# The order in which sixteen experts are traced: the next expert's gate and up products between the steps of the present one's activation

## The chip, the cores and the metric

One program runs on one core of a Trainium2 chip. The metric is the device time of one execution in microseconds. Lower is better.

## What is computed

The reference is a trunk of two layers over 512 tokens of width 1024. Each layer has a mixer (attention and a state space scan in layer 0, a chunked mLSTM in layer 1), a layer norm, a mixture of experts and a second layer norm. The change lies in the mixture and in the norm behind it:

```python
def hier_moe(x, w_group, b_group, w_expert, b_expert, w_gate, w_up, w_down):
    ...
    # one of 4 groups, then the best 2 of its 4 experts, weights normalised
    combine = jnp.einsum('tk,tke->te', weights, one_hot(expert_id, 16))
    hid = silu(einsum('td,edf->tef', t, w_gate)) * einsum('td,edf->tef', t, w_up)
    hid = hid * combine[:, :, None]
    return einsum('tef,efd->td', hid, w_down)

h = layer_norm(DN_ALPHA * h + ffn, ln_g[layer, 1], ln_b[layer, 1])   # DN_ALPHA = 4 ** 0.25
```

An expert has a hidden width of 256. All matrices are f32. The kernel splits each operand into a high and a low part, and a product is three matmuls (high with high, high with low, low with high).

## The kernel before

Each matrix of weights is cut into pieces of 128 x 2048 f32, 1 MB. An expert has three: piece 3e (gate and up columns, first half of the 1024 inputs), piece 3e+1 (second half) and piece 3e+2 (down). `load_piece` brings a piece by one DMA from SP's queue into a staging buffer (`raw`, `raw2`, or one of two `ca`), ScalarE (ACT) casts it to the high part (L213), and VectorE (DVE) or GpSimd (POOL) subtracts to get the low part (L214). Both parts lie in one of two pairs of slots `wh`/`wl` or one of two pairs `x8`/`x8`. `moe_piece(base, i, j)` picks these by the place j in the order of use: the pair by j mod 2; the staging buffer in the cycle raw, ca, ca (`raw2` for j = 3). POOL gets the subtraction by the piece's number i, not by its place: down pieces (i mod 3 = 2) below 42, and pieces 42 and 45.

`route` ranks the experts for one block of 128 tokens at a time, four blocks in all, with a chain of small DVE instructions (L897 to L963). While it works on the last block, the first four pieces of the mixture are already loaded and split, in the gaps of the engines' queues. Piece 2 is the third of them (j = 2) and so POOL's.

`experts` then loops over the 16 experts. Tokens of an expert are collected by a product with a 0/1 matrix, the dispatch, for a pair of experts at a time in four steps of 16 matmuls (`pair_parts`, L1070). A step fills one of the two PSUM buffers `tp`, which ACT (cast) and DVE (subtraction) then empty into `s2` or `xr`. An expert's work as it is traced:

- `gate_up(e)`: pieces 3e and 3e+1, 24 matmuls into a PSUM buffer `pj`
- two of the four dispatch steps of the next pair
- `hidden`: tanh on ACT (L1025), two DVE instructions (L1026, L1027), two transposes on TensorE (L1030) into `sm`
- the split of the transposed hidden values into two `pt` buffers (L213 on ACT, L214 on DVE)
- piece 3e+2 and 12 down matmuls into two `mm` buffers, ACT scales by the routing weight (L1177), ACT's queue writes the rows to `yd` in HBM (L1181)

Experts 14 and 15 stay on chip and are added by matmuls with transposed masks (L1279). After expert 13's write, `gather` makes alpha times x1 in `xr` out of its two parts (L1193 on ACT, L1194 on DVE) and issues eight indirect DMAs from POOL, which fetch the rows of the other experts and add them to `xr` (L1198). Then follow L1281 (adds the product of 14 and 15) and the layer norm (`ln_sums`).

A planner turns the traced program into one fixed order for each engine: at each moment of its own simulated time it takes, of the instructions that are ready, the one that was traced first. What the engines then do late by its reckoning, the queue behind it does late too.

Of the kernel before, what the change touches and what calls it, by code (L numbers as in the profile page):

```python
# [9 lines left out]
F32 = mybir.dt.float32  # L10
# [3 lines left out]
AF = mybir.ActivationFunctionType  # L14
# [6 lines left out]
EPS = 1e-5  # L21
# [30 lines left out]
class Trunk:  # L52
# [249 lines left out]
    def ln_sums(self, y, s, gb, pool):  # L302
# [13 lines left out]
        V.tensor_scalar(ve, ve, EPS, None, op0=ALU.add)  # L316
# [567 lines left out]
    def route(self, tb, layer, gb, lT, mu, rs, first):  # L884
# [78 lines left out]
        V.tensor_scalar(se, se, es, None, op0=ALU.mult)  # L963
# [57 lines left out]
    def hidden(self, gu):  # L1021

        nc = self.nc
        th = self.t("t", [128, 256])
        nc.scalar.activation(th, gu[:, 0:256], AF.Tanh, scale=0.5)  # L1025
        nc.vector.scalar_tensor_tensor(th, th, 1.0, gu[:, 0:256], op0=ALU.add, op1=ALU.mult)  # L1026
        nc.vector.scalar_tensor_tensor(th, th, 0.5, gu[:, 256:512], op0=ALU.mult, op1=ALU.mult)  # L1027
        tp = self.p("sm", [128, 2, 128])
        for k in range(2):
            nc.tensor.transpose(tp[:, k, :], th[:, k * 128:(k + 1) * 128], self.ident)  # L1030
        return tp
# [93 lines left out]
    def experts(self, layer):  # L1125
# [16 lines left out]
        def gate_up(e):  # L1142
            es = slice((e % 2) * 128, (e % 2 + 1) * 128)
            gus[e] = gu = self.p("pj", [128, 512])
            for q in range(2):
                w = self.moe_piece(base, 3 * e + q, next(used))
                for k in range(4):
                    xk = xs[e // 2][q * 4 + k]
                    self.mm3(gu, xk, w, q == 0 and k == 0, q == 1 and k == 3, np.s_[:, es], np.s_[:, k, :])

        for e in range(16):
# [3 lines left out]
            if e < 15:  # L1155
                gate_up(e)
            if e == 14:
                gate_up(15)
            for _ in range(2):
                next(prep, None)  # L1160
            tp = self.hidden(gus.pop(e))
            hT = (self.t("pt", [128, 2, 128], F32R), self.t("pt", [128, 2, 128], F32R))
            self.split(hT[0], hT[1], tp)
            w = self.moe_piece(base, 3 * e + 2, next(used))
# [22 lines left out]

    def gather(self):

        nc = self.nc  # L1190
        for tb in range(4):
            self.xr[tb] = self.t("xr", [128, 1024])
            nc.scalar.activation(self.xr[tb], self.xs[tb][0].bitcast(F32), AF.Copy, scale=ALPHA)  # L1193
            nc.vector.scalar_tensor_tensor(self.xr[tb], self.xs[tb][1].bitcast(F32), ALPHA, self.xr[tb],  # L1194
                                           op0=ALU.mult, op1=ALU.add)
# [400 lines left out]
```

## Time and profile before

| | us |
|---|---|
| median of 3 runs | 1133.4 (1129.15 to 1139.74) |
| profiled execution, its own time | 1130.67 |
| its span, first to last instruction | 1128.9 |
| mean granted TensorE clock over the span | 0.962 |

The profiled execution is the one whose rows are shown below; times in rows are microseconds from the start of the span. In the engine names PE is TensorE's matmul and PEld its weight load.

### The profile page before, as it was taken

The numbers are of one execution on the slowest core, as the hardware profiler recorded it, in microseconds if no ns is written. First come the engines' busy times: TensorE is split into PE (matmuls) and PEld (weight loads), VectorE is DVE, ScalarE is ACT, GpSimd is POOL, SyncE is SP. The second block draws the span as 40 slices with busy tenths as digits, with TensorE's granted clock in tenths as the row PEclk, the third lists the DMA queues.
The fourth block names the chain that finished last, engine by engine and source line by source line (L and its number), as shares of the span: only waits on it lengthen the run. The fifth ranks groups of instructions, "written<-read, shape, count | busy, mean of one in ns | idle before, by whom it ended". The sixth has DMA issues, their size and how long they took to land. (4 is left out here: it accounts for less than half of the span.)

```text
span 1128.9 us, 14811 instructions
## 1 busy us (share of the span) xinstructions
PE 1020.7 (90%) x5522; PEld 826.5 (73%) x5522; DVE 817.8 (72%) x1483; ACT 559.3 (50%) x778; POOL 394.6 (35%) x228
## 2 busy tenths in 40 slices
PE   8879999999979999987699999999999799999872
PEld 6576767767768877775577989898777688878761
DVE  7886899688776766667665766667988767667666
ACT  5223554461446666564544444444424467656644
POOL 3177545001343333346233333331014333424352
PEclk9889999999989999998898999999999899999986
DMA  6313321441356887768622222221413468868685
GB/s 227 109 55 111 122 74 37 171 168 39 117 191 244 302 291 260 278 217 248 140 75 75 76 75 75 75 75 38 150 38 138 149 244 314 291 220 311 224 219 135
DMA packets 48347, 180.62 MB, mean 160 GB/s; under 512 B 17588, under 2 KB 18516, under 8 KB 32264
## 3 DMA queue, kind: packets, MB, share of 16 engines
q1 hardware_dynamic: 41240, 156.11, 39.5%
q0 software_dynamic: 2992, 8.77, 4.0%
q10 hardware_dynamic: 4032, 14.68, 3.2%
q8 instruction: 46, 0.75, 0.3%
q14 instruction: 37, 0.30, 0.1%
HBM read 155.94 MB, written 22.42 MB: 158 GB/s over the span
## 5 line engine op out<-in xcount | busy, mean ns | idle before, releaser
L214 POOL TENSOR_TENSOR wl<-ca,wh 128x2048 fp32r<-128x2048 f32 x18 | 85.0, 4722 | 118.8 <-ACT wh L213 104.8
L265 PE MATMUL pj<-x,wh 128*128 128x512 f32 x288 | 116.8, 406 | 7.4 <-ACT x L213 5.5
L214 POOL TENSOR_TENSOR wl<-raw,wh 128x2048 fp32r<-128x2048 f32 x15 | 69.9, 4663 | 138.2 <-ACT wh L213 138.2
L266 PE MATMUL pj<-x,wh 128*128 128x512 f32 x288 | 115.7, 402 | 0.0
L213 ACT CAST wh<-raw 128x2048 fp32r<-128x2048 f32 (+1 forms) x49 | 88.2, 1800 | 54.6 <-DMA raw<-in_w 41.7
L267 PE MATMUL pj<-x,wl 128*128 128x512 f32 x288 | 115.1, 400 | 0.0
L1070 PEld LDWEIGHTS tp<-t,a 128*128 128x128 f32 x896 | 110.8, 191 | 3.0 <-ACT pt L1062 0.6
L1070 PE MATMUL tp<-t,a 128*128 128x256 f32 x896 | 111.8, 283 | 0.0
L214 POOL TENSOR_TENSOR x<-ca,x 128x2048 fp32r<-128x2048 f32 x14 | 64.5, 4610 | 125.8 <-ACT x L213 92.5
L214 DVE TENSOR_TENSOR wl<-raw,wh 128x2048 fp32r<-128x2048 f32 (+1 forms) x34 | 72.7, 2140 | 43.0 <-ACT wh L213 43.0
L1177 ACT ACTIVATE a<-mm,s5bc 128x512 f32<-128x512 f32 x56 | 38.5, 687 | 72.7 <-PE mm L267 72.7
L213 ACT CAST x<-ca 128x2048 fp32r<-128x2048 f32 (+1 forms) x40 | 66.1, 1652 | 11.5 <-DMA ca<-in_w 7.5
L214 DVE TENSOR_TENSOR wl<-ca,wh 128x2048 fp32r<-128x2048 f32 x12 | 27.5, 2293 | 59.7 <-ACT wh L213 59.7
L265 PEld LDWEIGHTS pj<-x,wh 128*128 128x128 f32 x288 | 55.4, 192 | 19.5 <-ACT x L213 6.3
L266 PEld LDWEIGHTS pj<-x,wh 128*128 128x128 f32 x288 | 55.1, 191 | 12.0 <-DVE x L214 1.6
L267 PEld LDWEIGHTS pj<-x,wl 128*128 128x128 f32 x288 | 55.2, 192 | 10.6
L213 ACT CAST wh<-ca 128x2048 fp32r<-128x2048 f32 x30 | 57.1, 1903 | 8.1 <-DMA ca<-in_w 7.8
L1051 DVE TENSOR_SCALAR t<-iota,rcm 128x128 fp32r<-128x128 f32 x112 | 57.2, 555 | 1.0 <-DMA cd<-rse,rpos 0.9
L280 POOL TENSOR_TENSOR lnrs<-lnve,nhalf 128x1 f32<-128x1 f32 x16 | 13.1, 818 | 125.7 <-DVE lnve L291 99.7
L266 PE MATMUL pj<-wl,x 128*128 128x256 f32 x192 | 56.2, 293 | 0.9 <-DVE wl L214 0.9
L265 PE MATMUL pj<-wh,x 128*128 128x256 f32 x192 | 56.3, 293 | 0.0
L267 PE MATMUL pj<-wh,x 128*128 128x256 f32 x192 | 56.1, 292 | 0.1
(488 smaller groups left out, 2880.5 us busy)
## 6 DMA issues: line engine op xcount, KB each, us to landing
raw<-in_w SPq DMA_DIRECT2D x63, 1024.0 KB, 5.5
ca<-in_w SPq DMA_DIRECT2D x62, 1024.0 KB, 5.7
yd<-a ACTq DMA_DIRECT2D x28, 512.0 KB
a<-in_ln SPq DMA_DIRECT2D x8, 512.0 KB, 6.4
a<-in_w SPq DMA_DIRECT2D x6, 512.0 KB, 6.5
yd<-t SPq DMA_DIRECT2D x6, 512.0 KB, 3.0
ca<-in_xT SPq DMA_DIRECT2D x8, 256.0 KB, 5.5
xr<-in_x SPq DMA_DIRECT2D x4, 512.0 KB, 6.3
```

What stands on the lines that cost most here:

```text
L213: a = nc.scalar.copy(h, src)
L214: b = (eng or nc.vector).tensor_sub(l, src, h.bitcast(F32))
L265: nc.tensor.matmul(ps, lhsT=aH[ai], rhs=bH[bi], start=first, stop=False)
L266: nc.tensor.matmul(ps, lhsT=aH[ai], rhs=bL[bi], start=False, stop=False)
L267: nc.tensor.matmul(ps, lhsT=aL[ai], rhs=bH[bi], start=False, stop=last)
L280: self.last_pow = self.nc.gpsimd.tensor_tensor(rs, ve, self.nhalf, op=ALU.pow)
L1051: ins = nc.vector.tensor_scalar(oh[:, j, m * 128:(m + 1) * 128], self.iota1, c[2 * i + j], None, op0=ALU.is_equal)
L1070: nc.tensor.matmul(tp[:, k, :], lhsT=self.xs[tb][i][:, cs], rhs=ohs[tb], start=tb + i == 0, stop=tb + i == 4)
L1177: nc.scalar.activation(yo[:, ns], ps, AF.Copy, scale=c)
```

## The change

The loop is traced in another order. At expert e the activation of e (L1025 to L1027) comes first, then dispatch steps of the next pair (three at even e, one at odd e), then the first half of `gate_up(e + 1)`, then the transposes and the split for e, the second half of `gate_up(e + 1)`, and the down product of e. The pieces are loaded in the order 0, 1, 3, 4, 2, 6, 7, 5, 9 and so on. x1 is rejoined from its two parts by one DVE addition per block, two traced at expert 12 and two at expert 13, without alpha; the routing weights are divided by alpha instead, and the norm's epsilon by alpha squared.

```diff
-        V.tensor_scalar(ve, ve, EPS, None, op0=ALU.add)
+        V.tensor_scalar(ve, ve, EPS / ALPHA ** 2, None, op0=ALU.add)
...
-        V.tensor_scalar(se, se, es, None, op0=ALU.mult)
+        V.tensor_scalar(se, se, es, 1.0 / ALPHA, op0=ALU.mult, op1=ALU.mult)
...
     def hidden(self, gu):
+        return self.hidden_T(self.hidden_act(gu))
+
+    def hidden_act(self, gu):
...
+        return th
+
+    def hidden_T(self, th):
         tp = self.p("sm", [128, 2, 128])
...
             for q in range(2):
+                if q:
+                    yield
                 w = self.moe_piece(base, 3 * e + q, next(used))
...
-            if e < 15:
-                gate_up(e)
-            if e == 14:
-                gate_up(15)
-            for _ in range(2):
+            if e == 0:
+                list(gate_up(0))
+            th = self.hidden_act(gus.pop(e))
+            for _ in range(1 if e % 2 else 3):
                 next(prep, None)
-            tp = self.hidden(gus.pop(e))
+
+            ahead = gate_up(e + 1) if e < 15 else iter(())
+            next(ahead, None)
+            tp = self.hidden_T(th)
             hT = (self.t("pt", [128, 2, 128], F32R), self.t("pt", [128, 2, 128], F32R))
             self.split(hT[0], hT[1], tp)
+            list(ahead)
+            if e in (12, 13):
+                for tb in (2 * e - 24, 2 * e - 23):
+                    self.rejoin(tb)
             w = self.moe_piece(base, 3 * e + 2, next(used))
...
+    def rejoin(self, tb):
+        self.xr[tb] = self.t("xr", [128, 1024])
+        self.nc.vector.tensor_tensor(self.xr[tb], self.xs[tb][0].bitcast(F32), self.xs[tb][1].bitcast(F32), op=ALU.add)
+
     def gather(self):
         nc = self.nc
-        for tb in range(4):
-            self.xr[tb] = self.t("xr", [128, 1024])
-            nc.scalar.activation(self.xr[tb], self.xs[tb][0].bitcast(F32), AF.Copy, scale=ALPHA)
-            nc.vector.scalar_tensor_tensor(self.xr[tb], self.xs[tb][1].bitcast(F32), ALPHA, self.xr[tb],
-                                           op0=ALU.mult, op1=ALU.add)
```

## Rows read from the trace of the kernel before

**Rows 1.** The page, part 1: busy us, share of the span, instructions of each engine.

```profile
PE 1020.7 (90%) x5522; PEld 826.5 (73%) x5522; DVE 817.8 (72%) x1483; ACT 559.3 (50%) x778; POOL 394.6 (35%) x228
```

**Rows 2.** One expert as a window: length, busy us (instructions) by engine, clock, DMA, GB/s.

```profile
353.70:366.10 12.40, 12.40 (x71) 10.66 (x70) 6.56 (x8) 7.78 (x9) 4.62 (x1) 1.00 0.72 242
```

**Rows 3.** TensorE's waits in layer 0's mixture: us in total, times, longest.

```profile
PE mm L267 <- DVE pt L214: 4.9, 3, 2.1
...
PE sm L1030 <- DVE t L1027: 3.9, 3, 1.7
```

**Rows 4.** Timeline of TensorE, both layers: start us, us, line, tiles, count, [idle before].

```profile
327.76 3.98 PE L1070 MATMUL tp<-t,a 128*128 128x256 f32 x32
...
331.72 0.48 PE L265 MATMUL pj<-x,xr 128*128 128x512 f32 x1
...
337.41 0.40 PE L265 MATMUL pj<-wh,xr 128*128 128x512 f32 x1
...
340.21 3.98 PE L1070 MATMUL tp<-t,a 128*128 128x256 f32 x32
...
488.44 1.03 PE L1059 MATMUL tp<-ident,t 128*128 128x128 f32 x8
...
502.69 3.98 PE L1070 MATMUL tp<-t,a 128*128 128x256 f32 x32
...
890.91 3.98 PE L1070 MATMUL tp<-t,a 128*128 128x256 f32 x32
...
1065.24 3.98 PE L1070 MATMUL tp<-t,a 128*128 128x256 f32 x32
```

**Rows 5.** Timeline of the last block's routing, layer 0, then layer 1.

```profile
306.91 2.29 DVE L214 TENSOR_TENSOR x<-ca,x 128x2048 fp32r<-128x2048 f32 x1
307.27 6.32 POOL L214 TENSOR_TENSOR wl<-ca,wh 128x2048 fp32r<-128x2048 f32 x1 [1.84 <-DMA cd<-rse,rpos]
...
309.11 4.57 DVE L906 TENSOR_TENSOR rgt<-rlg 128x80 bf16<-128x80 f32 x1
...
871.45 0.23 DVE L906 TENSOR_TENSOR rgt<-rlg 128x80 bf16<-128x80 f32 x1
...
871.88 5.17 DVE L908 TENSOR_TENSOR req<-req,low 128x80 bf16<-128x80 bf16 x1
872.47 4.51 POOL L214 TENSOR_TENSOR wl<-ca,wh 128x2048 fp32r<-128x2048 f32 x1
```

**Rows 6.** Timeline around expert 13 and the gather, layer 0, then layer 1.

```profile
501.94 4.80 DVE L1194 SCALAR_TENSOR_TENSOR xr<-a,xr 128x1024 f32<-128x1024 f32 x1 [5.82 <-ACT xr L1193]
...
514.36 1.90 ACT L213 CAST x<-ca 128x2048 fp32r<-128x2048 f32 x1
...
516.88 0.33 ACTq L1181 DMA_DIRECT2D yd<-a  x1
...
1079.42 0.33 ACTq L1181 DMA_DIRECT2D yd<-a  x1
...
1110.34 0.69 DVE L1281 SCALAR_TENSOR_TENSOR xr<-pj,xr 128x512 f32<-128x512 f32 x1 [0.73 <-DMA xr<-yd,rsrc]
```

**Rows 7.** Timeline of one staging buffer that carries down pieces, layer 0.

```profile
384.13 4.61 POOL L214 TENSOR_TENSOR x<-ca,x 128x2048 fp32r<-128x2048 f32 x1 [8.37 <-ACT x L213]
...
388.77 4.35 SPq L247 DMA_DIRECT2D ca<-in_w  x2
...
396.93 4.62 POOL L214 TENSOR_TENSOR wl<-ca,wh 128x2048 fp32r<-128x2048 f32 x1 [8.19 <-ACT wh L213]
```

**Rows 8.** Timeline of the emptying of two dispatch steps, layer 0.

```profile
343.20 0.69 DVE L214 TENSOR_TENSOR s<-tp,s 128x512 fp32r<-128x512 f32 x1
...
458.04 3.98 PE L1070 MATMUL tp<-t,a 128*128 128x256 f32 x32
...
463.16 1.90 ACT L213 CAST x<-ca 128x2048 fp32r<-128x2048 f32 x1 [2.30 <-DMA ca<-in_w]
...
465.57 1.29 DVE L214 TENSOR_TENSOR xr<-tp,xr 128x512 fp32r<-128x512 f32 x2 [1.89 <-ACT xr L213]
```

More of the change, by code (lines that the diff above doesn't have):

```diff
@@ L1027, in hidden @@
         nc.vector.scalar_tensor_tensor(th, th, 0.5, gu[:, 256:512], op0=ALU.mult, op1=ALU.mult)
+        return th
+    def hidden_T(self, th):
         tp = self.p("sm", [128, 2, 128])
         for k in range(2):
-            nc.tensor.transpose(tp[:, k, :], th[:, k * 128:(k + 1) * 128], self.ident)
+            self.nc.tensor.transpose(tp[:, k, :], th[:, k * 128:(k + 1) * 128], self.ident)
         return tp
```

## The prediction

> **What bounds the kernel now.** I read the page first: TensorE is busy for 90% of the span [rows 1], so whatever gains must remove its idle time, or a chain on which it waits. Next I asked where that idle time lies. The windows show an expert without a stall: 12.40 us, all of it busy [rows 2]. TensorE's timeline gives the same work as it comes in practice. From the first dispatch of the loop to expert 13's, 13 experts, layer 0 takes 502.69 - 327.76 = 174.93 us and layer 1 takes 1065.24 - 890.91 = 174.33 [rows 4]. Thirteen unstalled experts are 13 x 12.40 = 161.2, and the last pair adds 1.03 for its transposed masks [rows 4]. So stalls and the refilling after them cost **12.7 us in layer 0 and 12.1 in layer 1**. The waits name their cause: TensorE wants the hidden values split (pt) or the activation done (t) and DVE is late [rows 3].
>
> Then I looked at the end of each mixture. From expert 13's write to the last gathered block in layer 1 is 1110.34 - 1079.42 = 30.9 us [rows 6]; TensorE has less left to do than that. So what counts at the end of a mixture is the moment of expert 13's write.
>
> Last, the routing of the fourth block, ahead of each mixture, is a chain of DVE instructions of which one is far too long: L906 takes 4.57 us in layer 0 and 0.23 in layer 1, where its like L908 takes 5.17 [rows 5]. Each of the long ones ends with POOL's subtraction for piece 2 (307.27 + 6.32 = 313.59; 872.47 + 4.51 = 876.98). DVE stood still while POOL worked.
>
> **The change, part by part.**
>
> *Routing.* The third piece loaded is now piece 3, which is not POOL's. Piece 2 comes as the fifth, when its slot is freed by expert 0's first products, behind the routing. That takes 4.57 - 0.23 = 4.34 us off the chain in layer 0 and 5.17 - 0.23 = 4.94 in layer 1 [rows 5], together 9.3. But DVE now has a subtraction of 2.29 us more at this time. The second piece's already stands in the middle of the chain (306.91, [rows 5]), since the planner fills gaps with what is ready. If piece 3's falls there too, it costs 2 x 2.29 = 4.6; if it falls behind the chain, nothing. I have no row that decides, and take half: **-7.0, bounds -9.3 to -4.7**.
>
> The Trainium skill, Perfetto Trace Analysis, section Optimizing Scalar/DVE Operations, speaks against this part: VectorE and GpSimd share a read port of SBUF, so shifting work between them might not help. By that rule this term would be 0 and the sum -9.8. The rows agree that the two engines hold each other up, but also show that the price here is POOL's whole instruction against DVE's shorter one.
>
> *The stalls between the steps.* The activation of e is now followed on TensorE by the down product of e - 1, one or three dispatch steps and half of the next gate and up product before the transposes. Twelve matmuls take 340.21 - 337.41 = 2.80 us [rows 4], a dispatch step 3.98 / 2 = 1.99 [rows 4]. Thus T(e), the transposes, come at least 2.80 + 1.99 + 2.80 = 7.6 us after the activation can start; that wait should vanish. The split of the hidden values has the second half, 2.80 us, as its cover, and the waits for it were 4.9 in all, three times [rows 3]; I leave 0.5 us of them per layer.
>
> Two new limits come instead.
>
> First, at even e three dispatch steps follow each other through two PSUM buffers. The third waits until the first is emptied, and has the 1.99 us of the second step for it. A quick emptying ends 343.20 + 0.69 - (340.21 + 1.99) = 1.7 us after its step [rows 4, 8]: no wait. A slow one starts at 465.57 and ends about 6.2 us after its step (458.04 + 1.99), since ACT stood behind a cast that waited for a load [rows 8]: a wait of 4.2. These are the fastest and slowest kind of the 14 first steps of layer 0; I worked out all from the timeline, and the mean excess over 1.99 is 1.1 us. With seven pairs that is 7.9 per layer, unless the planner, seeing the buffer full, runs the gate and up matmuls first. I take half, **4.0 per layer (0 to 7.9)**.
>
> Second, the loads. A down piece holds its staging buffer for a load, a cast, POOL's subtraction. Before, in one `ca`, that cycle was 396.93 - 384.13 = 12.80 us, of which the next load started (388.77) as POOL ended (388.74) [rows 7]. Now all down pieces go through the single `raw`. The cycle is as long, but an unstalled expert is 12.40, so it falls behind by 0.4 x 13 = 5.2 us over a layer, and the slot for down piece e is now free only when `gate_up(e)` is done, which leaves a lead of 2.8 + 2.0 + 5.6 + 0.3 - 6.6 = 4 us at odd e (down product, dispatch, products, transposes, less cast and POOL). Lead and lag nearly cancel; with some late landings I take **3 us per layer (0 to 22, the rival below)**.
>
> Left of the 24.8 us: 2 x (0.5 + 4.0 + 3.0) = 15.0. Gain **-9.8, bounds -23.8 to +19**.
>
> *Expert 13's write.* Before, 13 or so of expert 14's 24 matmuls ran ahead of the write; now all must, 11 more at 2.80 / 12 = 0.233: +2.6 us. Against this, the stretch from dispatch to write was 516.88 - 502.69 = 14.19 [rows 4, 6], and now it is dispatch and transposes 4.0, products 5.6, down 2.8, scaling and issue 1.0 (516.88 - 514.36 - 1.90 = 0.6, [rows 6], and the way from the last matmul) = 13.4. The cast of 1.90 us in ACT's queue ahead of the last scaling [rows 6] may return. I take **0, bounds -0.8 to +1.2 per layer**. Behind the write the gather is as it was.
>
> *Rejoining.* Four ACT instructions go, and four DVE instructions are replaced by four of one size. The first took 4.80 [rows 6], again behind POOL, and held up the activation of 13, a wait that is part of the 12.7. Now the additions lie at 12 and 13, behind the products that read the same `xr` buffers, with a whole expert until the gather. A second factor in one tiny instruction and another constant cost nothing: same count and shapes.
>
> *Sum.* -7.0 - 9.8 + 0 = -16.8. The profiled execution takes 1130.67, so 1113.9 by its own time. It lies 2.7 below the median of the runs, within their spread; on the median's scale 1133.4 - 16.8 = **1116.6, said as 1117**.
>
> **The rivals.**
>
> *All is covered.* The planner hides the third step, the loads keep up, the moved subtraction lies behind the routing: -23.8 - 9.3 - 1.6 = -34.7, 1099. For it: 13 of TensorE's experts could run at 12.40. Against: every engine's queue is fixed by planned times, and DVE is held by POOL's 4.6 us once per expert. Band 1099 to 1110.
>
> *The third step eats the gain.* 7.9 instead of 4.0, and 5 instead of 3 for the loads, per layer: stalls left 2 x 13.4 = 26.8, so +2.0, and with a routing gain of 4.7 to 7.0 the time is 1128 to 1131. For it: the mean of the rows as they are.
>
> *The loads become the bound (slower).* One `raw` for down pieces, with POOL's subtraction inside its cycle. If landing and waiting for the cast grow by 1.7 us, the cycle is 14.5 against 13.46 per expert now (174.93 / 13, [rows 4]): 13 x 1.04 = 13.5, less the lead of about 4, +9.5 per layer; with the routing's -7 that is +12, 1145. It decides from a cycle of some 13.9 on. For it: ACT's cast was seen to wait 2.30 us for a load [rows 8]. Against: the same cycle was run at 12.80 before.
>
> *The change does not do what it says.* The planner already starts the next products while the present activation waits (331.72, before expert 0's down product, [rows 4]). If its order hardly changes, only the routing's part is left: -4.7 to -9.3, 1124 to 1129.
>
> *The routing gains nothing.* By the mechanism that DVE is busy where POOL was: -9.8, 1123.6.
>
> **How the numbers follow.** Forecast (1110 to 1122) 0.42; all covered 0.12; third step 0.20; loads 0.10; order unchanged 0.10; no gain in routing 0.06. About 1% is what a measurement of this kernel can tell from no change: faster is below 1122.1, slower above 1144.7. Faster: 0.42 + 0.12 and a little of the rest, 0.56. Slower: half of the loads' case and some chance for what I didn't see, 0.08. The range for 8 in 10 leaves out the best of the covered case and the loads' case: 1101 to 1138.
>
> **What would show it.** In the changed profile: L906 and L908 of the last block at about 0.2 us each, no subtraction on POOL beside them, and the mixture starting 2 to 5 us sooner. Dispatch starts of two successive experts together nearer to 25 us than to 26.9. No wait of TensorE for t or pt over 1 us. If the third step bites, waits of L1070 for DVE's subtraction from tp at even experts; if the loads bite, waits of pj or mm matmuls for POOL's low parts, and a cycle of `raw` above 13 us. The prediction is wrong if the write of expert 13 comes later, from the loop's first dispatch, than 189 us (516.88 - 327.76), or if DVE's added subtraction stands in the routing chain and something else there is late.

## The result, and the profile after

The changed kernel takes **1191.0 us** (median of 4 runs, 1189.21 to 1193.23) against 1136.2 for the kernel before (4 runs, three of them those of the table ahead of the prediction): a ratio of 1.0475, 95% interval 1.0434 to 1.0517. The forecast was 1117 with a range up to 1138, so both the sign and the range were wrong. The profiled execution takes 1192.37 us, with a span of 1190.7 (before 1130.67 and 1128.9) and a mean granted clock of 0.936 (before 0.962).

Part 1 of the page, as [rows 1]: TensorE is busy longer and yet for a smaller share.

```profile
PE 1042.5 (88%) x5522; PEld 847.7 (71%) x5522; DVE 818.6 (69%) x1483; ACT 554.2 (47%) x770; POOL 394.8 (33%) x228
```

The two loops over the experts as windows, from the first dispatch to expert 13's write (length, busy us of PE, PEld, DVE, ACT, POOL with instructions, granted clock, DMA share, GB/s), in the changed kernel and then in the kernel before:

```profile
332.10:550.90 218.80, 189.57 (x996) 160.69 (x995) 135.49 (x158) 121.19 (x129) 77.27 (x17) 0.94 0.64 234
925.70:1144.70 219.00, 190.74 (x996) 162.73 (x995) 140.56 (x158) 121.32 (x129) 76.44 (x16) 0.92 0.63 233
```

```profile
327.80:516.90 189.10, 175.83 (x979) 148.23 (x977) 126.22 (x148) 122.12 (x131) 69.78 (x16) 1.00 0.72 259
```

The loop takes 29.7 us more in layer 0. TensorE's idle time in it went from 189.10 - 175.83 = 13.3 to 218.80 - 189.57 = 29.2, and its busy time grew by 13.7: 17 matmuls more ahead of the write (996 against 979) make some 4 us of that at the 0.233 of a matmul, the clock most of the rest, 0.94 in place of 1.00. All that was lost lies in the mixtures. With the start of L907 (L906 before), the first step of the first and of the last pair and expert 13's write as marks, the span's 61.8 us divide so:

| stretch, us | before, layer 0 and 1 | after | difference |
| --- | --- | --- | --- |
| first rank instruction to the first dispatch | 18.65, 19.46 | 22.92, 23.32 | +4.3, +3.9 |
| six pairs of experts | 162.58, 161.98 | 178.48, 179.64 | +15.9, +17.7 |
| last pair's first step to 13's write | 26.54, 26.53 | 40.25, 39.31 | +13.7, +12.8 |
| write to the next layer's rank, to the end | 354.57, 49.5 | 351.54, 46.0 | -3.0, -3.5 |

The marks of layer 0 after are 309.20, 332.12, 510.60 and 550.85 in the next fence but one; those of layer 1 are 902.39, 925.71, 1105.35 and 1144.66. Those of before are in [rows 4 to 6], with 1052.90 for the last pair of layer 1 and, in layer 0, the last of these three rows (the first two are the way from the routing to the loop):

```profile
317.85 1.20 PE L1106 MATMUL pj<-pt,a 128*128 128x256 f32 x4 [1.30 <-DVE rpos L952]
...
322.05 0.51 PE L265 MATMUL pj<-wh,xr 128*128 128x512 f32 x1 [0.45 <-PEq L1208]
...
490.34 2.89 PE L1070 MATMUL tp<-t,a 128*128 128x256 f32 x22
```

The timeline of the changed kernel, layer 0: the routing, then the third of three steps at two pairs, then expert 13.

```profile
309.20 0.23 DVE L907 TENSOR_TENSOR rgt<-rlg 128x80 bf16<-128x80 f32 x1
...
309.58 2.28 DVE L214 TENSOR_TENSOR wl<-ca,wh 128x2048 fp32r<-128x2048 f32 x1
...
315.76 0.55 PE L1113 MATMUL pj<-pt,a 128*128 128x256 f32 x1 [1.31 <-DVE rpos L953]
319.93 0.98 PE L1113 MATMUL pj<-pt,a 128*128 128x256 f32 x3 [3.62 <-PEq L1223]
...
329.79 0.40 PE L265 MATMUL pj<-wh,xr 128*128 128x512 f32 x1
...
332.12 0.63 PE L1077 MATMUL tp<-t,a 128*128 128x256 f32 x4
...
386.00 2.28 DVE L214 TENSOR_TENSOR x<-ca,x 128x2048 fp32r<-128x2048 f32 x1
386.29 3.99 PE L1077 MATMUL tp<-t,a 128*128 128x256 f32 x32
386.68 6.08 POOL L214 TENSOR_TENSOR wl<-raw,wh 128x2048 fp32r<-128x2048 f32 x1 [7.04 <-ACT wh L213]
...
390.02 1.91 ACT L213 CAST x<-ca 128x2048 fp32r<-128x2048 f32 x1 [2.32 <-DMA ca<-in_w]
391.96 2.94 DVE L214 TENSOR_TENSOR x<-ca,x 128x2048 fp32r<-128x2048 f32 x1 [3.67 <-ACT x L213]
394.83 1.27 DVE L214 TENSOR_TENSOR s<-tp,s 128x512 fp32r<-128x512 f32 x2
395.56 2.64 PE L1077 MATMUL tp<-t,a 128*128 128x256 f32 x16 [3.43 <-DVE s L214]
...
419.06 4.59 POOL L214 TENSOR_TENSOR wl<-raw,wh 128x2048 fp32r<-128x2048 f32 x1 [9.37 <-ACT wh L213]
421.45 4.35 DVE L214 TENSOR_TENSOR x<-ca,x 128x2048 fp32r<-128x2048 f32 x1 [4.20 <-ACT x L213]
...
510.60 2.18 PE L1077 MATMUL tp<-t,a 128*128 128x256 f32 x16 [0.47 <-ACT pt L1069]
...
533.22 5.35 POOL L214 TENSOR_TENSOR wl<-ca,wh 128x2048 fp32r<-128x2048 f32 x1
534.42 5.22 DVE L1206 TENSOR_TENSOR xr<-a,a 128x1024 f32<-128x1024 f32 x1
539.57 0.41 DVE L1031 SCALAR_TENSOR_TENSOR t<-t,pj 128x256 f32<-128x256 f32 x1
540.03 0.44 PE L1037 MATMUL sm<-ident,t 128*128 128x128 f32 x2 [4.72 <-DVE t L1031]
...
550.85 0.33 ACTq L1196 DMA_DIRECT2D yd<-a  x1
```

Three things are to be seen, against [rows 5, 8, 6]. The rank chain is free of POOL (0.23 in place of 4.57), but the branch for overflowing experts (L1223) now stands behind the first of 16 matmuls and not behind all, and TensorE stops at it for 3.62 us (0.45 before). TensorE's branch instruction itself takes 3.4 and 3.7 us in both kernels; before, the 16 matmuls ran meanwhile. The third step waits 3.43 us for the emptying of the first. That emptying (394.83) stands behind a weight's subtraction on DVE (391.96), which stands behind a cast on ACT that waited 2.32 us for its load (390.02), and which POOL's subtraction holds for 0.65 us; at the next pair, and at two more, POOL holds it for 2.1 us (4.35 at 421.45 in place of 2.28). And expert 13's transposes wait 4.72 us for an activation that stands behind an addition of the rejoining, which POOL's subtraction holds (534.42 + 5.22 = 539.64, POOL's ends at 538.57).

TensorE's waits from 290 to 560 us (releaser: us in total, times, longest), as [rows 3]:

```profile
PE tp L1077 <- DVE xr L214: 7.7, 2, 4.3
PE tp L1077 <- DVE s L214: 6.8, 2, 3.4
PE sm L1037 <- DVE t L1031: 5.8, 2, 4.7
PE mm L265 <- ACT pt L213: 4.1, 1, 4.1
PE tp L1077 <- DVE t L1058: 3.8, 1, 3.8
```

The waits of [rows 3], 4.9 us for pt and 2.3 of the 3.9 for t in the six pairs, are down to 0.5 and 1.1 there (the other 4.7 us for t and the 4.1 for pt belong to experts 13 and 12), nearly as forecast. In their place stand the dispatch matmuls' waits for DVE, of 3.4 to 4.3 us, and what follows each: the granted clock, in windows around the third step at 395.56.

```profile
393.00:396.80 3.80, 1.24 (x10) 1.24 (x11) 3.10 (x3) 0.00 (x0) 0.00 (x0) 1.00 0.76 276
396.80:400.40 3.60, 3.60 (x15) 3.10 (x14) 0.69 (x1) 0.62 (x2) 0.00 (x0) 0.53 1.01 419
```

So a stall like this one costs twice, by itself and by a clock near its lower level (1.2 GHz, 0.5 in these rows) behind it.

### The profile page after: what moved, and what is told of

The parts are those of the page before. It is cut to its first block, busy times and chain, and to the rows that moved or that the text cites. A ratio compares the mean times of both kernels' runs of the same rounds, so it can differ in the third digit from the quotient of the medians.

```text
span 1190.7 us, 14814 instructions
## 1 busy us (share of the span) xinstructions
PE 1042.5 (88%) x5522; PEld 847.7 (71%) x5522; DVE 818.6 (69%) x1483; ACT 554.2 (47%) x770; POOL 394.8 (33%) x228
## 5 line engine op out<-in xcount | busy, mean ns | idle before, releaser
L214 POOL TENSOR_TENSOR wl<-raw,wh 128x2048 fp32r<-128x2048 f32 x29 | 142.6, 4916 | 244.2 <-ACT wh L213 220.5
L1077 PE MATMUL tp<-t,a 128*128 128x256 f32 x896 | 129.6, 303 | 38.2 <-DVE s L214 13.7
L1077 PEld LDWEIGHTS tp<-t,a 128*128 128x128 f32 x896 | 125.1, 209 | 46.0 <-DVE s L214 15.5
L214 POOL TENSOR_TENSOR x<-raw,x 128x2048 fp32r<-128x2048 f32 x14 | 66.1, 4720 | 166.9 <-ACT x L213 166.9
L214 DVE TENSOR_TENSOR x<-ca,x 128x2048 fp32r<-128x2048 f32 (+1 forms) x38 | 88.7, 2337 | 25.3 <-ACT x L213 25.3
L214 DVE TENSOR_TENSOR wl<-ca,wh 128x2048 fp32r<-128x2048 f32 x28 | 70.5, 2517 | 47.7 <-ACT wh L213 47.7
L266 PEld LDWEIGHTS pj<-x,wh 128*128 128x128 f32 x288 | 54.9, 191 | 12.1 <-DVE x L214 1.8
L280 POOL TENSOR_TENSOR lnrs<-lnve,nhalf 128x1 f32<-128x1 f32 x16 | 12.7, 795 | 121.4 <-DVE lnve L291 98.4
L1360 DVE SCALAR_TENSOR_TENSOR t<-pj,cw,t 128x511 f32<-128x511 f32 (+2 forms) x48 | 35.9, 747 | 21.7 <-ACT t L1358 20.9
L214 DVE TENSOR_TENSOR wl<-raw,wh 128x2048 fp32r<-128x2048 f32 (+1 forms) x20 | 40.7, 2034 | 13.3 <-ACT wh L213 13.2
L966 POOL DMA_INDIRECT cd<-rse,rpos x16 | 20.4, 1275 | 78.7 <-DVE rpos L953 61.7
```

The lines of the kernel that those rows point to most:

```text
L214: b = (eng or nc.vector).tensor_sub(l, src, h.bitcast(F32))
L266: nc.tensor.matmul(ps, lhsT=aH[ai], rhs=bL[bi], start=False, stop=False)
L280: self.last_pow = self.nc.gpsimd.tensor_tensor(rs, ve, self.nhalf, op=ALU.pow)
L966: ins = nc.gpsimd.indirect_dma_start(out=self.cd[:, :], out_offset=bass.IndirectOffsetOnAxis(ap=pos[:, r:r + 1], axis=0), in_=se, in_offse ...
L1077: nc.tensor.matmul(tp[:, k, :], lhsT=self.xs[tb][i][:, cs], rhs=ohs[tb], start=tb + i == 0, stop=tb + i == 4)
L1360: V.scalar_tensor_tensor(y[:, d:], ps[:, :512 - d], self.cw[:, i, 3 - d:4 - d], y[:, d:], op0=ALU.mult, op1=ALU.add)
```

## The experiments

Ratios, with the 95% interval, are to the kernel before, run beside each group of runs; its medians there were 1134 to 1136 us. Code is cut at each "...". All figures per pair and per layer are worked out from the timeline as in the table above.

**First: the step, its buffer, the loads.** The waits that the trace shows are those for the emptying of tp, so theory 1 was the third step, theory 2 the loads in their new order and buffers, theory 3 the casts ahead of the emptying in the queues of ACT and DVE.

Two steps at each expert again:

```diff
-            for _ in range(1 if e % 2 else 3):
+            for _ in range(2):
```

> The changed kernel, but with two dispatch steps at each expert, as before, in place of three at even and one at odd experts. Theory 1 (the third step waits for the first step's buffer): the waits of 3.4 to 4.3 us of the dispatch matmuls for the emptying of tp, and the half clock behind each, vanish at all seven pairs; some 5 to 6 us a pair come back, 30 to 35 us a layer at most, 1125 to 1140 us. Theory 2 (the loads and the staging of the pieces are late in the new order, and the step only shows it): the lateness moves to the next matmul that needs a piece, 1175 to 1190 us. Theory 3 (the emptying stands in ACT's and DVE's queues behind weight casts whose loads land late; it matters only where TensorE has nothing else to do): like theory 1, but with some waits left, 1135 to 1155 us.

Measured: 1190.0 us, 1.0487 (1.0407 to 1.0567). The waits for the emptying are gone and the time has not moved, as theory 2 had it. TensorE's waits in this run's first loop:

```profile
PE tp L1077 <- DVE t L1058: 17.0, 5, 3.4
PE tp L1066 <- DVE t L1058: 7.9, 1, 7.9
```

L1058 makes the **masks** of a pair, eight small DVE instructions. Six of the seven pairs now wait for them, five at the dispatch and the last at its transposed masks (L1066). Theory 1 falls, and theory 3 with it, although its chain is in the rows above (390.02 to 395.56): the wait that the trace showed was only one of several things that were late.

The third step into another PSUM buffer:

```diff
-            tp = self.p("tp", [128, ks, n])
+            tp = self.p(tags[q], [128, ks, n])      # tags: tp, tp, sm, tp
...
```

> The changed kernel, but the third of the four dispatch steps writes to the PSUM buffers of the transposes (sm) and not to tp, so three steps in a row no longer share two buffers. Theory 1: the waits of the third step vanish, 1135 to 1155 us. Theory 2: the time stays at 1175 to 1190 us. Theory 3: the third step does not wait any more, but what comes behind it does, the transposes (which use sm) or the products that read the pair's x, since the same emptying is still queued behind casts: 1155 to 1175 us.

Measured: 1177.5 us, 1.0355 (1.0276 to 1.0434). A quarter of the loss comes back; three waits for masks and two of the products for the emptying take the place of the rest.

Each kind of piece staged where it was before:

```diff
-                               "raw2" if j == 3 else self.MOE_RAW[(j - (j > 3)) % 3], at=base + i,
+                               "raw2" if j == 3 else ("raw" if j == 0 else "ca" if j < 3 else ("ca", "raw", "ca")[i % 3]), at=base + i,
```

> The changed kernel, but each kind of piece is staged where it was before: the up pieces in raw, the gate and down pieces in ca; the order of the loads stays the new one. Theory 2: the cycle of the down pieces (load, cast, POOL's subtraction) no longer runs through one buffer, the loads land earlier and the emptying with them: 1140 to 1165 us. Theory 1: unchanged within 1%, 1180 to 1200 us. Theory 3: a few us either way, 1175 to 1200 us.

Measured: 1187.2 us, 1.046 (1.038 to 1.0539). The staging is worth nothing that can be told. The new order of the loads, the other half of theory 2, falls too: runs below keep it and take 1136 us.

The kernel before with three and one steps:

```diff
-            for _ in range(2):
+            for _ in range(1 if e % 2 else 3):
```

> The kernel before, with one part of the change alone: three dispatch steps at even and one at odd experts in place of two at each. Theory 1: the third step waits here too, some 4 us and a stretch of half clock at each pair: 1160 to 1195 us. Theory 2: 1130 to 1140 us, since order and staging of the loads are the old ones. Theory 3: in between, 1140 to 1165 us, as fewer emptyings stand behind late casts in the old order.

Measured: 1139.1 us, 1.004 (0.9996 to 1.0084): not told from no change. Theory 1 had 1160 at least.

**Second: the masks.** With the activation traced ahead of the steps, the masks of a pair, which its first step issues, come behind the activation in DVE's queue. From the end of the last mask to the fifth matmul of the first step, which is the first to read the second half of them, the changed kernel has 0.2 to 0.7 us at four of layer 0's seven pairs and 2.8 at the last; at the first two they are late by 0.7 and 4.1. Before the change the margin was 2.1 to 6.9 us at all seven. This is theory 4.

The activation back behind the steps, with three and one, and with two steps:

```diff
-            th = self.hidden_act(gus.pop(e))
             for _ in range(1 if e % 2 else 3):      # and, in the second run, range(2)
                 next(prep, None)
+            th = self.hidden_act(gus.pop(e))
```

> The changed kernel, with the activation of expert e traced behind its one or three dispatch steps, where it stood before the change, and the two halves of the next products still around the transposes. Theory 4 (new, after the first runs: with the activation traced first, the masks of a pair and the emptying of tp come to DVE and ACT only when TensorE already needs them, and any hold there, behind POOL's subtraction or a cast, stops TensorE): the masks are ready some 2 to 7 us ahead again as before the change, most of the waits and of the half clock go, 1130 to 1155 us. Theory 2 (staging and loads): no change, 1180 to 1195 us. Theory 1 (the third step) has been refuted as the main cause by the run with two steps at each expert; what is left of it would show here as waits of some 2 us at even experts.

Measured: 1159.1 us, 1.0203 (1.0163 to 1.0243): most of the loss is gone, though it is 4 us above theory 4's range.

> As the run with the activation behind the steps, and with two dispatch steps at each expert. Theory 4: also 1130 to 1155 us, within 10 us of that run. Theory 2: 1180 to 1195 us. If the third step still costs what the kernel before with three and one steps showed (some 5 us in all), this one is faster by that.

Measured: 1135.7 us, 1.001 (0.9976 to 1.0043); a pair takes 26.2 us in layer 0 against 27.1 before (157.24 / 6 and 162.58 / 6). So the order is worth 32 us with three steps and 54 with two, and the third step costs 23 us once the masks are in time. In the run with three steps its waits are these:

```profile
PE tp L1077 <- DVE xr L214: 4.6, 3, 1.8
PE tp L1077 <- DVE s L214: 4.5, 3, 1.7
```

Here too the emptying stands behind a weight's subtraction on DVE that runs beside POOL's and takes 3.6 to 4.3 us in place of 2.28, once at each of the six pairs.

The masks traced one expert earlier, the activation left where the change has it:

```diff
...
             for _ in range(1 if e % 2 else 3):      # and, in a later run, range(2)
                 next(prep, None)
+            if e % 2 and e < 13:
+                self.pair_masks((e + 3) // 2)
```

> The changed kernel with the activation left ahead of the steps, but the eight mask instructions of a pair traced one expert earlier, behind the last step of the pair before. Theory 4 in its narrow form (the late masks are the cause): the waits for t (masks) vanish and with them most of the loss, 1135 to 1160 us. Theory 4 in its wide form (the emptying of tp, behind the activation in the same queues, is as late as the masks): the waits for the emptying at the third step stay or grow in place of those for the masks, 1165 to 1190 us. Theory 2: 1180 to 1195 us.

Measured: 1159.5 us, 1.0201 (1.0162 to 1.024), the same as with the activation behind the steps. The later run:

> The changed kernel with the activation left ahead of the steps, the masks of a pair traced one expert earlier, and two steps at each expert. The runs so far: masks behind the activation with two steps 1190, with three and one steps 1191; masks early or activation behind with three and one steps 1159; activation behind with two steps 1136. Theory 4, narrow (the order activation ahead of steps costs only through the late masks): the same as with the activation behind the steps, 1130 to 1142 us, and a pair of experts in about 25.9 us. Theory 4, wide (the emptying of tp is late as well behind the activation): 1145 to 1165 us, with waits for the emptying.

Measured: 1136.1 us, 1.0001 (0.9966 to 1.0036). The narrow form holds: what the order costs, it costs through the masks.

The kernel before with the activation ahead of the steps, and nothing else (`hidden` is split into its two halves for it, as in the change):

```diff
+            th = self.hidden_act(gus.pop(e))
             for _ in range(2):
                 next(prep, None)
-            tp = self.hidden(gus.pop(e))
+            tp = self.hidden_T(th)
```

> The kernel before with one edit of the change alone: the activation (tanh and its two products) traced ahead of the two dispatch steps, the transposes behind them. Theory 4: this edit alone carries most of the loss, 1160 to 1190 us, with waits of the dispatch matmuls for masks or for the emptying of tp. If the loss needs the half products around the transposes or the new order of the loads as well: within 1% of before, 1125 to 1145 us.

Measured: 1184.9 us, 1.0442 (1.0387 to 1.0497). One line moved carries 50 us. Its timeline at the fifth pair:

```profile
457.49 0.28 DVE L1057 TENSOR_SCALAR t<-iota,rcm 128x128 fp32r<-128x128 f32 x1
...
458.02 5.72 DVE L1057 TENSOR_SCALAR t<-iota,rcm 128x128 fp32r<-128x128 f32 x7
458.68 4.58 POOL L214 TENSOR_TENSOR x<-ca,x 128x2048 fp32r<-128x2048 f32 x1 [7.26 <-ACT x L213]
...
463.39 4.85 PE L1076 MATMUL tp<-t,a 128*128 128x256 f32 x26 [3.80 <-DVE t L1057]
```

One mask takes 0.28 us, seven should take about 1.5, and take 5.72: DVE stands until POOL's subtraction ends (458.68 + 4.58 = 463.26), and TensorE starts again at 463.39. The sixth pair's seven masks take 5.72 us as well. Before the change it was the same at the sixth pair, a group of four masks of 3.73 us beside a subtraction on POOL, but dispatch came only at 458.04 [rows 8]:

```profile
450.68 4.63 POOL L214 TENSOR_TENSOR wl<-ca,wh 128x2048 fp32r<-128x2048 f32 x1 [7.93 <-ACT wh L213]
...
452.26 3.73 DVE L1051 TENSOR_SCALAR t<-iota,rcm 128x128 fp32r<-128x128 f32 x4
```

**Third: POOL's subtraction as the price.** In the run just told, the subtractions that meet the masks are those of the odd experts' down pieces. They go to DVE:

```diff
-                               eng=self.nc.gpsimd if i % 3 == 2 and i < 42 or i in (42, 45) else None,
+                               eng=self.nc.gpsimd if i % 6 == 2 and i < 42 or i in (42, 45) else None,
```

> The kernel before with the activation ahead of the steps (1185 us in its run, a pair's masks held until the end of a subtraction of 4.6 us on POOL), and with the odd experts' down pieces subtracted by DVE in place of POOL: it is their subtraction that stands beside the masks there. Theory L (DVE stands still while POOL's subtraction runs; masks that come late cost 3.8 us only because of that): the eight masks take 2 to 3 us in place of 5.7, TensorE's wait for them goes or is under 1 us, 1140 to 1165 us, though DVE has 7 subtractions of 2.29 us more a layer. Theory Q (the masks are late by DVE's own queue): the waits stay and DVE's added work makes them longer, 1180 to 1200 us.

Measured: 1119.6 us, 0.9839 (0.9761 to 0.9917), 65 us faster than without this edit, and faster than the kernel before; it lies below theory L's own range too. Its timeline at the sixth pair, and the first loop as a window, here and in the run without the edit:

```profile
465.02 1.46 DVE L1057 TENSOR_SCALAR t<-iota,rcm 128x128 fp32r<-128x128 f32 x7
...
465.67 4.08 PE L1076 MATMUL tp<-t,a 128*128 128x256 f32 x32
```

```profile
334.20:512.20 178.00, 172.96 (x960) 146.26 (x960) 120.25 (x160) 118.14 (x128) 33.76 (x9) 0.99 0.75 269
```

```profile
339.30:545.60 206.30, 179.28 (x956) 153.41 (x955) 130.03 (x153) 118.20 (x128) 63.74 (x15) 0.95 0.64 232
```

Seven masks take 1.46 us, though they are still made just in time. DVE has seven subtractions more and is shown busy for 120 us and not 130: the difference was standing still. Theory L holds in its mechanism, theory Q falls. One rival lies near: DVE's subtraction takes 2.29 us and POOL's 4.6, so a staging buffer comes free sooner for the next load. It is not that: ACT's waits for loads in the six pairs of layer 0 are 7.7 us without this edit and 9.4 with it.

The same in the changed kernel itself, where it is the even experts' pieces that meet the masks and the emptying (386.68 above):

```diff
-                               eng=self.nc.gpsimd if i % 3 == 2 and i < 42 or i in (42, 45) else None,
+                               eng=self.nc.gpsimd if i % 6 == 5 and i < 42 or i in (42, 45) else None,
```

> The changed kernel with nothing else but the even experts' down pieces subtracted by DVE in place of POOL; it is theirs, of 4.6 to 6.1 us, that stand beside the masks and the emptying of tp in its trace. Theory L (POOL's subtraction beside work of DVE that TensorE waits for is the price; the activation ahead of the steps only made that work late enough to feel it): 1125 to 1150 us, the waits of the third step mostly gone. Theory T (three steps in a row through two buffers remain, 23 us with masks in time): some of it stays, 1140 to 1160 us. If the lock were only part of it: 1165 to 1185 us.

Measured: 1136.5 us, 1.0022 (0.9995 to 1.0049). Of the change's 55 us, 54 are gone. ACT's waits for loads are 13.1 and 12.1 us, so again it is not the loads. No wait for the masks is left in the six pairs of layer 0, the stretch from the last pair's first step to the write is 28.13 and 29.61 us in place of 40.25 and 39.31, and the third step's waits, in the same window as above, are down from 14.5 to 4.5 us:

```profile
PE tp L1077 <- DVE s L214: 3.2, 2, 1.8
...
PE tp L1077 <- DVE xr L214: 1.3, 1, 1.3
```

So most of the third step's 23 us are not its own: the six pairs take 159.98 and 160.60 us here, against 169.27 and 168.78 with three steps and 157.24 and 157.78 with two, the activation behind them. The stops of 1.3 to 1.8 us left the clock at 1.00 over these six pairs.

**Fourth: the rejoining, the write of 13, the branch.** Expert 13's write came 33.1 us after the last pair's first step in the run with the activation behind two steps, against 26.5 before. Is it the early additions (theory A) or the products of 14 ahead of it (theory B)? The rejoining alone in the kernel before:

```diff
...
-            nc.scalar.activation(self.xr[tb], self.xs[tb][0].bitcast(F32), AF.Copy, scale=ALPHA)
-            nc.vector.scalar_tensor_tensor(self.xr[tb], self.xs[tb][1].bitcast(F32), ALPHA, self.xr[tb],
-                                           op0=ALU.mult, op1=ALU.add)
...
+            if e in (12, 13):
+                for tb in (2 * e - 24, 2 * e - 23):
+                    self.rejoin(tb)
```

> The kernel before with the rejoining part of the change alone: one addition each on DVE at experts 12 and 13, the results over alpha, no scaling on ACT. Theory A: the write of expert 13 is later by 2 to 6 us a layer from the first dispatch, 1138 to 1146 us. Theory B: unchanged or a little faster, 1128 to 1137 us, since four casts of ACT go.

Measured: 1144.4 us, 1.0058 (1.0028 to 1.0088); the last stretch is 33.96 and 34.35 us against 26.53. Behind the write it is 5.6 and 1.2 us shorter than before, so only some 9 us reach the time. Two additions of 5.3 us each, beside two subtractions on POOL, stand ahead of the activation of 13:

```profile
514.22 10.63 DVE L1194 TENSOR_TENSOR xr<-a,a 128x1024 f32<-128x1024 f32 x2 [0.44 <-PE pj L266]
...
528.96 0.69 PE L1030 MATMUL sm<-ident,t 128*128 128x128 f32 x2 [7.57 <-DVE t L1027]
```

The additions traced at the gather again, in the run with the activation behind two steps:

```diff
-            if e in (12, 13):
-                for tb in (2 * e - 24, 2 * e - 23):
-                    self.rejoin(tb)
...
+        for tb in range(4):
+            self.rejoin(tb)
```

> Activation behind the steps, two steps at each expert, and the four additions that rejoin x1 traced at the gather again, behind expert 13, still as one addition each on DVE. Theory A (the early additions at 12 and 13 cost: in the run without this edit a pair takes 25.9 us against 26.9 before, but expert 13's write comes 33.1 us behind the last pair's first step against 26.5 before): the last pair loses most of the 6.5 us, twice, 1122 to 1130 us. Theory B (the last pair is late for another reason, the transposed masks or the products of 14 traced ahead of the write): unchanged, 1133 to 1139 us.

Measured: 1137.8 us, 1.0018 (0.998 to 1.0056). This tells nothing: the planner put the additions in the old place, one of 5.26 us still ahead of the activation's second product.

Held by an added dependency behind the split of 13's hidden values; then, besides, with 14's products traced behind the write:

```diff
-            self.split(hT[0], hT[1], tp)
+            low = self.split(hT[0], hT[1], tp)[1]
...
+            if e == 13:
+                for tb in range(4):
+                    self.rejoin(tb, [low])      # after(..., [low])
```

> The run with the activation behind the steps and two steps each, and the four additions of the rejoining held behind the split of expert 13's hidden values (traced at the gather alone, the planner had put two of them, 5.30 and 5.26 us each behind POOL, ahead of that expert's activation all the same). Theory A: TensorE's wait of 3.4 us for the activation of 13 goes, and the write of 13 comes 3 to 6 us sooner per layer: 1126 to 1133 us. Theory B (the last pair is late by the products of 14 ahead of the write): 1133 to 1140 us.

Measured: 1131.9 us, 0.997 (0.9935 to 1.0006); the last stretch falls from 33.10 and 34.66 to 28.46 and 28.44.

```diff
-            next(ahead, None)
+            if e != 13:
+                next(ahead, None)
...
-            list(ahead)
+            if e != 13:
+                list(ahead)
...
                 nc.scalar.dma_start(yd[e], yo)
+            list(ahead)
```

> As the run with the additions held behind expert 13's split, and expert 14's products traced behind the write of 13, so the planner need not have all 24 of them ahead of it. Theory B: the write comes 3 to 6 us sooner than in that run, 3 to 10 us off the time. Theory A alone: no change, within 3 us of that run.

Measured: 1127.6 us, 0.989 (0.9813 to 0.9968); the last stretch is 23.05 and 23.08. Both theories have a part in the moment of the write: 4.6 and 6.2 us for the additions, 5.4 in each layer for the products (131 matmuls in the stretch and not 155). But the products then lie behind the write: from there to the next layer's rank and to the end it is 354.28 and 53.25 us in place of 349.31 and 48.71, and the spans of the two profiled executions, 1131.1 and 1129.8, differ by 1.3 us. The medians differ by 4.3, of 4 runs (1123 to 1132) and 10 (1127 to 1134). What the products' place is worth in time is thus not settled. In the kernel before, the dependency behind 13's split:

> The kernel before with the rejoining in one addition and the results over alpha, the additions held behind the split of expert 13's hidden values (placed at experts 12 and 13 as the change has them, the same edit took 1144 us against 1135). Theory A: the loss of that run goes, and the wait for the first of the four in the kernel before (4.80 us) as well, 1125 to 1134 us. If the loss came from the missing casts of ACT or from the gather, it stays: 1140 to 1148 us.

Measured: 1137.3 us, 0.9993 (0.9945 to 1.004): the loss of the early additions goes, nothing is gained, and the time lies between the two ranges.

The branch traced behind the rest of the first pair's dispatch (with the additions at the gather):

```diff
-        self.overflow(layer, base)
         for _ in self.pair_parts(0, x):
             pass
+        self.overflow(layer, base)
```

> As the run with the additions at the gather, and the branch for overflowing experts traced behind the rest of the first pair's dispatch instead of ahead of it. Theory C (the branch can only be taken some 6 us behind the count's matmul, since its register is loaded then; the changed kernel's queue has it ahead of 15 of the 16 matmuls that would fill this time, so the routing's gain of 2.2 and 2.8 us is lost): the first dispatch of each loop comes 2 to 4 us sooner, 4 to 8 us off that run's time. Theory D (the way to the loop is set by something else, the masks or the first products' pieces): no change within 2 us.

Measured: 1138.7 us, 1.0022 (0.9996 to 1.0048), no faster than the run it starts from. From the first rank instruction to the first dispatch it took 22.65 and 17.79 us against 20.71 and 23.92: layer 1 gains 6.1, layer 0 loses 1.9, where one of the masks is held for 4.63 us. TensorE still stops at the branch for 4.05 and 2.08 us, though all 16 matmuls and six products now stand ahead of it: it ends 11.0 and 8.4 us behind the count's matmul, so theory C's 6 us are no fixed time. Inconclusive: the branch's place does matter, but the time does not follow.

**Last: the parts that gained, together.** Activation behind two steps, additions behind 13's split, the write of 13 first, and the odd experts' down pieces subtracted by DVE:

> The run with the activation behind the steps, two steps each, the additions behind expert 13's split and the write of 13 ahead of 14's products, and with the odd experts' down pieces subtracted by DVE, since in its trace theirs (4.63 us) hold a mask and with it the activation's second product. Theory L: a pair goes from 25.9 to some 25.0 to 25.4 us, 6 to 10 us off that run: 1113 to 1123 us, faster than both kernels. If DVE's added 7 x 2.29 us a layer weigh as much as the lock: 1124 to 1132 us.

Measured: 1115.3 us, 0.9847 (0.9811 to 0.9883), the lowest median of all. A pair takes 25.3 us (151.79 / 6); the first loop as a window:

```profile
330.70:505.50 174.80, 173.25 (x980) 150.17 (x979) 132.13 (x153) 119.30 (x128) 41.90 (x10) 1.00 0.78 283
```

TensorE is idle for 1.6 us of it, against 13.3 before.

## Why the prediction was wrong

**What bounds the kernel** was read rightly: the 12 or so us of stalls per layer are there to be had, and the last run has them (its loops are 14.3 and 12.5 us shorter, with as many matmuls). That "what counts at the end of a mixture is the moment of expert 13's write" is true in part only: with 14's products behind the write it came 5.4 us sooner in each layer, and 5.0 and 4.5 us were lost again behind it.

**The stalls between the steps** (-9.8, bounds to +19) is the term that failed: the six pairs alone grew by 15.9 and 17.7 us, +33.6. (Its upper bound is that of the loads alone; with the 0.5 and 7.9 us that it names beside their 22 it would have been +36.) The step in it that failed is the first: the order "activation, down product, one or three steps, half of the products, transposes" was costed by TensorE's matmuls and by the emptying of tp. The masks, which the first step issues on DVE, had no place in the sum. So the wait for the activation did nearly vanish (1.1 us in the six pairs of layer 0), and the activation, now first in DVE's queue, pushed the masks to the last moment. That alone would have been harmless (1120 us in the kernel before with the activation ahead and the odd pieces' subtractions off POOL, 1136 in the changed kernel with the even ones off it). The second half of the cause stood in the prediction, as "DVE is held by POOL's 4.6 us once per expert", but as a reason against the best case, with no price: it was nowhere asked on whose path those 4.6 us would fall. They fell on TensorE's, through the masks or through the weight's subtraction ahead of the emptying, in stops of over 3 us at five of the seven pairs in each layer, with the clock behind them.

**The third step** was mis-sized. I took 4.0 us a layer, at most 7.9. With the masks late it costs nothing (1191 against 1190), since the masks' wait takes its place; with the masks in time it costs 23 us in all, 11.7 a layer; in the kernel before some 5 in all, within the noise. Most of that price hangs on whether POOL holds the subtraction ahead of the emptying. In the result the sign I had named for it, waits of the dispatch matmuls for the emptying, appeared as forecast and was not the cause.

**The loads** (3 us a layer, and the rival that was to end slower, 1145) are worth nothing: the old staging gives 1187 against 1191. The one rival that would have ended slower had the wrong mechanism, and slower had a chance of 0.08 in all.

**The routing** (-7.0, bounds -9.3 to -4.7): the chain from its first rank instruction to the first L1113 matmul went from 317.85 - 309.11 = 8.74 to 315.76 - 309.20 = 6.56 and from 9.39 to 6.57, -5.0 in all, with the moved subtraction inside the chain as the half that I feared. But the planner moved the branch, and the first dispatch comes 4.3 and 3.9 us later: +13 between the chain's end and that dispatch that the sum did not have. The rows tell it apart: from the first of the 16 matmuls to expert 0's first product it takes 3.30 us more in each layer, by the stops of 3.62 and 3.75 us at the branch; expert 0's 24 products take 0.8 and 1.1 us more; and ten products of expert 1 (329.79 to 332.12, 2.33 us) now run ahead of the first dispatch, which is work moved and not lost.

**Expert 13's write** (0, bounds -0.8 to +1.2) was +13.7 and +12.8. The sum had 11 matmuls more ahead of the write, 2.6 us; there are 25 (154 against 129 in this stretch; the six pairs have nine fewer), products of 14 and of 15, 5.8 us at 0.233. TensorE's idle time in the stretch grew by 5.1 and 3.8 us (it holds 4.7 us for 13's activation, and 4.1 and 2.8 for 12's split hidden values), and the rest, some 3 us, is the clock (0.92 and 0.87 in place of 1.00).

**The rejoining** (0) puts off the write by 7.4 and 7.8 us by itself, and costs some 9 us in all. The cover I named, "a whole expert until the gather", is the gather's; the additions stand in DVE's queue, beside two subtractions on POOL, ahead of 13's activation. The row that should have warned is in [rows 6]: the old one took 4.80 us for the same reason. Nor was the wait behind it, 1.6 us, "part of the 12.7": TensorE's wait ends at 509.19, behind the 502.69 up to which the 12.7 are counted.

The rule of the Trainium skill weighed in the prediction (Perfetto Trace Analysis, Optimizing Scalar/DVE Operations: shifting work between VectorE and GpSimd might not help, as they share a port) bears on more than the routing. Here the trace goes further: taking half of the subtractions away from POOL made the kernel before with the activation ahead faster by 65 us, and the changed kernel by 54. The rival worked out beside it, no gain in the routing, fell as well: the chain did get shorter, by 5.0 us.

## What to carry to other kernels

When work is moved ahead in a program, list every instruction of every engine that now comes behind it, the small ones above all, and ask how long before its use each was ready. A wait in the trace names the last of several things that are late; taking it away shows whether it was the cause. Where two engines exclude each other, price the longer one's whole instruction on whatever the shorter one would have done then, and ask whether TensorE waits for that.

## What the runs showed of the hardware

DVE is not held in all it does while POOL subtracts. In the run with the write of 13 first, inside one subtraction on POOL, the activation's first product, which reads PSUM and one SBUF operand, took 0.42 us as ever, and the mask behind it, which reads SBUF alone, 4.19:

```profile
427.32 4.63 POOL L214 TENSOR_TENSOR x<-raw,x 128x2048 fp32r<-128x2048 f32 x1 [7.43 <-ACT x L213]
427.50 0.42 DVE L1030 SCALAR_TENSOR_TENSOR t<-t,pj 128x256 f32<-128x256 f32 x1 [0.22 <-ACT t L1029]
427.84 4.19 DVE L1058 TENSOR_SCALAR t<-iota,rcm 128x128 fp32r<-128x128 f32 x1
```

The Trainium skill (SBUF — State Buffer, Who interferes with whom) says that a DVE instruction with at most one SBUF input, outside the modes that use both ports, does not contend with GpSimd, and that a tensor_scalar can enter such a mode; these rows agree. So an emptying of PSUM, which reads PSUM and one SBUF operand as well, is not held itself: in the kernel before, two of them took 1.29 us at 465.57 [rows 8], beside a subtraction on POOL from 465.19 to 469.77, and 1.27 at 394.83 in the changed kernel, where POOL had ended. It was late where a weight's subtraction stood ahead of it in the queue. It goes the other way too: POOL's subtraction of 4.6 us took 6.08 at 386.68, where a DVE subtraction of 2.28 had begun 0.68 us earlier. And after a stop of TensorE of 3.43 us, which ended at 395.56, the granted clock was still 1.00 up to 396.80 and 0.53 from there to 400.40.
